# A hymba layer on one core: the job order of the attention projections, the queue of the backward scan's reloads, and the first two products

## The chip, the core and the metric

The kernel runs on one core of a Trainium2 chip. The metric is device microseconds (us) of one execution. Before the change three runs gave a median of 1325.76 us (1324.9 to 1326.83).

## What is computed

One encoder layer on 2048 tokens of width 1024, in float32. A single projection of the input feeds two mixers: neighbourhood attention with 8 heads on a grid of 32 rows and 64 columns, and a gated linear recurrence (HGRN2) with 4 heads that runs over the tokens in both directions. Both results are gated, put side by side, projected once more and added to the input, and a LayerNorm follows. Cut to that, the reference reads:

```python
h = jnp.einsum('btd,de->bte', x, w_in) + b_in
q_a, k_a, v_a, g_a, q_h, z_fwd, z_bwd, i_h, g_h = jnp.split(h, split_at, axis=-1)
o_a = neighbourhood_attention(heads_a(q_a), heads_a(k_a), heads_a(v_a), rpb)
o_a = o_a * jax.nn.silu(g_a)
logf_f, k_f = hgrn2_forget(heads_h(z_fwd), lb_fwd_logits, layer)
logf_b, k_b = hgrn2_forget(heads_h(z_bwd), lb_bwd_logits, layer)
o_fwd = hgrn2_chunk_scan(qh, k_f, ih, logf_f)
o_bwd = flip(hgrn2_chunk_scan(flip(qh), flip(k_b), flip(ih), flip(logf_b)))
o_h = rms_norm(o_fwd + o_bwd) * hg_norm_gain * jax.nn.silu(g_h)
y = jnp.einsum('bte,ed->btd', jnp.concatenate([o_a, o_h], axis=-1), w_out) + b_out
out = layer_norm(alpha * x + y)
```

## The kernel before

**Products.** Every float32 operand of a projection is split (`split`, L152) into a rounded high part, which ACT casts (L155), and a low part, which VectorE gets by a subtract (L156). A product is then three matmuls for each of 8 K-tiles: high by high, low by high, high by low. So a projection of one column chunk of 128 for one block of 512 tokens is 24 matmuls of 512 columns. The four value projections of a mixer go together in a wide job of 96 matmuls. All instructions of TensorE go through `mm` and `transpose` (L139, L142), which chain them in the order in which the code issues them.

**Units.** The tokens come in two halves of two blocks each (block 0 and 1, then 2 and 3). Each half has eight units: hg 0 to 3, one head of the recurrence each, then att 0 to 3, two heads of attention each. Numbered through they are n = 0 to 15; n = 8 to 11 are the hg units of the second half and n = 12 to 15 its attention units. An hg unit of the second half runs the forward scan, then the backward scan over all four blocks. For the blocks of the first half it reloads what it had stored in DRAM: `fetch` (L639 to L648) loads rQg, ub, op and rg, 256 KB each, for two blocks, by SP's queue. `hg_back` (L576) goes through a block in four steps: a matmul `pb` with the state `Sb`, and a step of `Sb` on VectorE (L586).

**Fillers.** The projections are not done in phases of their own. `projections` (L319) is a generator that yields after each matmul, and `advance` (L951) draws from it between the steps of the units, so that TensorE has work while other engines prepare the next step. Such a matmul is called a filler here; each half has 1728 of them, and 144 more come from the output projection (`out_first`, L914). The order of the fillers is that of the jobs (`half_jobs`, L282). How they spread is set by the table `marks` (L890): its entries say at which filler a unit starts, and within a unit the fillers are spread evenly over its steps (an attention unit of the second half has 45, three for each iteration). Weights are loaded by SP's queue and split when a job begins or the one ahead of it does (`prepare`, L323); at the start of the last job the first w_out tiles and features for the output product are loaded (`out_loads`, L910).

**An attention unit** has 12 items (`main`, L809). Each iteration does three things with fillers between them: the scores of an item (`scores`, L741: matmuls `S` of the split queries in `km` and `qm` and the split keys in `ST`, then the softmax on VectorE and ACT), the transposes `ptr` of the item two before (`turn`, L770), and on every second iteration the product with the values, `pov` (`weigh`, L784). Ahead of its first scores stand the splits of the queries and keys of its first group: `prep_q` (L698 to L709, casts on ACT, subtracts at L707 and L708 on VectorE) and `prep_k` (L716 to L723). For block 1 they read the reloads rq, r0k and r1k (L683 to L690, SP's queue). A unit checks whether it may start the splits of the next one (`ahead`, called at L821 from iteration 11 on, and at the end of hg units): that is when all q and k projections of the next unit have been issued.

**The start.** `first_loads` (L179) loads the weights of the chunks 16 (q) and 20 (zf) of the first hg unit and block 0 of the transposed input in halves of 256 columns; the first two products then run in two rounds of 256 columns, 96 matmuls in all (L341 to L352): all K-tiles of q, then all of zf, then both for the other half of the columns.

Of the kernel before, what the change touches and what calls it, by code (L numbers as in the profile page):

```python
# [11 lines left out]
F32 = mybir.dt.float32  # L12
F32R = mybir.dt.float32r
# [5 lines left out]
P = 128  # L19
# [3 lines left out]
TB = 512  # L23
NTB = T // TB
KT = D // P
ATT_HEADS, DH = 8, 64
HG_HEADS = 4
NCHUNK = 36
# [47 lines left out]
def _build():  # L76
    nc = _bacc.Bacc("TRN2", target_bir_lowering=False, num_devices=1, dynamic_dma_scratch_size=4096)

    def din(name, shape):
        return nc.dram_tensor("in_%s_dram" % name, shape, F32, kind="ExternalInput").ap()  # L80

    x_in = din("x", (T, D))
    xT_in = din("xT", (KT, P, T))
    w_in = din("w_in", (NCHUNK, P, KT, P))
    b_in = din("b_in", (P, NCHUNK))
    wv_in = din("w_v", (2, KT, P, 4 * P))
# [6 lines left out]
    out = nc.dram_tensor("out_0_dram", (T, D), F32, kind="ExternalOutput").ap()  # L93

    with tile.TileContext(nc) as tc, ExitStack() as top:
# [17 lines left out]
        def h_tile(name):  # L113
            return hp.tile([P, TB], F32, tag="h", name=name)
# [24 lines left out]
        def mm(out, lhsT, rhs, start, stop, **kw):  # L139
            in_order(nc.tensor.matmul(out, lhsT=lhsT, rhs=rhs, start=start, stop=stop, **kw))  # L140
# [10 lines left out]
        def split(dst, raw, scale=None):  # L151

            hi, lo = dst[:, 0], dst[:, 1]
            if scale is None:
                nc.scalar.copy(out=hi, in_=raw)  # L155
                last_split[0] = nc.vector.tensor_tensor(out=lo, in0=raw, in1=hi.bitcast(F32), op=ALU.subtract)  # L156
            else:
                nc.scalar.activation(hi, raw, AF.Copy, scale=scale)
                nc.vector.scalar_tensor_tensor(out=lo, in0=raw, scalar=scale, in1=hi.bitcast(F32), op0=ALU.mult, op1=ALU.subtract)
# [18 lines left out]

        def first_loads():  # L179


            wa = wp.tile([P, 2, KT, P], F32R, tag="w", name="wt")
            wraw = [rawp.tile([P, KT // 2, P], F32, tag="raw", name="wraw") for _ in range(2)]
            tiles = [xwp.tile([P, 2, TB], F32R, tag="xw", name="xt") for _ in range(KT)]

            def half(o, kt, n):
                cs = slice(o * 256, o * 256 + 256)
                raw = h_tile("xraw").rearrange("p (k t) -> p k t", k=2)
                nc.sync.dma_start(out=raw[:, 0:n], in_=xT_in[kt:kt + n, :, cs].rearrange("k p t -> p k t"))
                for k in range(n):  # L190
                    split(tiles[kt + k][:, :, cs], raw[:, k])

            for kt in range(0, KT, 2):
                part = wraw[kt // 4][:, kt % 4:kt % 4 + 2]
                nc.sync.dma_start(out=part, in_=w_in[16, :, kt:kt + 2])
                split(wa[:, :, kt:kt + 2], part)
                if kt == 0:
                    half(0, 0, 1)
                    half(0, 1, 1)
                else:  # L200
                    half(0, kt, 2)
            wb = load_w(20)
            for kt in range(0, KT, 2):
                half(1, kt, 2)
            return wa, wb, tiles

        def load_w(c):
            w = wp.tile([P, 2, KT, P], F32R, tag="w", name="wt")
            for i in range(2):
                raw = rawp.tile([P, KT // 2, P], F32, tag="raw", name="wraw")  # L210
                nc.sync.dma_start(out=raw, in_=w_in[c, :, i * 4:i * 4 + 4])
                split(w[:, :, i * 4:i * 4 + 4], raw, 0.125 if c < 4 else None)
            return w
# [66 lines left out]
        xts = {}  # L280

        def half_jobs(half):  # L282

            tbs = (0, 1) if half == 0 else (2, 3)
            first = 8 * half

            def both(u, *whats):
                hg = {"q": 16, "zf": 20, "zb": 24, "g": 32}
                att = {"q": 0, "k": 4, "g": 12}
                return [(first + u, what, (hg[what] + u) if u < 4 else (att[what] + u - 4), tb, (first + u, what))  # L290
                        for what in whats for tb in tbs]

            def wide(what, tb):
                return [(first, what, WIDE.index(what), tb, (what, tb))]

            jobs = both(0, "q", "zf", "zb")
            jobs[1], jobs[2] = jobs[2], jobs[1]
            jobs += wide("v4", tbs[0]) + wide("v4", tbs[1]) + both(0, "g")
            for u in (1, 2, 3):
                jobs += both(u, "q", "zf", "zb", "g")  # L300
            jobs += wide("a4", tbs[0]) + both(4, "q", "k") + wide("a4", tbs[1]) + both(4, "g")
            jobs += both(5, "q", "k", "g") + both(6, "q", "k", "g")
            end = both(7, "q", "k", "g")
            if half == 0:
                end[3], end[4] = end[4], end[3]
                return jobs + end
            end = [end[i] for i in (0, 2, 1, 3, 4, 5)]
            return jobs + [(n, what, c, tb, (n, what, tb)) for n, what, c, tb, _ in end]
# [10 lines left out]
        def projections():  # L319
# [18 lines left out]
            first_consts()  # L338
            prepare(jobs[2])
            banks = [ps_tile("pj", "pj"), ps_tile("pj", "pj")]  # L340
            for o in range(2):  # L341
                cs = slice(o * 256, o * 256 + 256)
                for ps, what in zip(banks, ("q", "zf")):
                    w = ws[0, what]
                    for kt in range(KT):
                        for i, (a, b) in enumerate(((0, 0), (1, 0), (0, 1))):
                            mm(ps[:, cs], w[:, a, kt], xts[0][kt][:, b, cs], kt == 0 and i == 0, kt == KT - 1 and i == 2)
                            if (kt * 3 + i) % 2 and not (o == 1 and kt == KT - 1 and i == 2):
                                yield 1
                    if o == 1:  # L350
                        gots[0][what, 0] = evac_plain(ps, 16) if what == "q" else evac_tanh(ps, 20)
                        yield 1  # L352
            for m, job in enumerate(jobs):
# [259 lines left out]
        def hg_unit(half, u, h, ahead):  # L613
# [25 lines left out]
            def fetch(tb):  # L639
                s = hg_saved[u, tb]  # L640
                Qg = h_tile("rQg")
                nc.sync.dma_start(out=Qg, in_=s["Qg"])
                ub = wk("ub", [P, 4, P], F32)
                nc.sync.dma_start(out=ub.rearrange("p a b -> p (a b)"), in_=s["ub"])
                op = wk("op", [P, 4, P], F32)
                nc.sync.dma_start(out=op.rearrange("p a b -> p (a b)"), in_=s["op"])
                g = h_tile("rg")
                nc.sync.dma_start(out=g, in_=gots[u]["g", tb])  # L648
                h["g", tb] = g
                rs[tb] = dict(Qg=Qg, ub=ub, op=op, dec=s["dec"])  # L650

# [236 lines left out]
        total = sum(job_size(job) for half in range(2) for job in half_jobs(half))  # L888
        half = total // 2
        marks = [240, 540, 772, 1004, 1240, 1425, 1610, 1795]  # L890
        marks += [half + 250, half + 540, half + 770, half + 1000, half + 1232, half + 1396, half + 1555, half + 1714, total + 144]

        def all_fillers():
            yield from projections()
# [240 lines left out]
```

## Time and profile before

| | us |
|---|---|
| median of 3 runs | 1325.76 |
| the profiled execution | 1326.96 |
| its span | 1325.2 |
| TensorE (PE) busy | 1300.8 |
| VectorE (DVE) busy | 877.9 |
| ScalarE (ACT) busy | 669.6 |
| GpSimd (POOL) busy | 92.0 |

What lies between the span and the execution's time is 1.8 us. Times are counted from the span's start. In the timeline a row is the start, the length, the engine, the line, the operation with its tiles and shapes, a count, and in brackets the idle time ahead of it with what ended it; SPq is SP's DMA queue. The end of a matmul is modelled, so a price is read from one start to the next. In the windows each engine has its busy time and instruction count, and behind them stand the granted TensorE clock (1.00 is full), the share of time that the DMA engines were busy, and GB/s. Groups give busy time and mean ns of one instruction, then the idle time ahead of them. DMA rows give the count, the size, and the median us from issue to landing.

TensorE is the busiest engine from the start to the end. From 1174 us on only the output product and the LayerNorm are left.

### The profile page before, as it was taken

The numbers are of one execution on the slowest core, as the hardware profiler recorded it, in microseconds if no ns is written. First come the engines' busy times: TensorE is split into PE (matmuls) and PEld (weight loads), VectorE is DVE, ScalarE is ACT, GpSimd is POOL, SyncE is SP. The second block draws the span as 40 slices with busy tenths as digits, with TensorE's granted clock in tenths as the row PEclk, the third lists the DMA queues.
The fourth block names the chain that finished last, engine by engine and source line by source line (L and its number), as shares of the span: only waits on it lengthen the run. The fifth ranks groups of instructions, "written<-read, shape, count | busy, mean of one in ns | idle before, by whom it ended". The sixth has DMA issues, their size and how long they took to land. (4 is left out here: it accounts for less than half of the span.)

```text
span 1325.2 us, 23230 instructions
## 1 busy us (share of the span) xinstructions
PE 1300.8 (98%) x8774; PEld 1088.3 (82%) x8774; DVE 877.9 (66%) x2078; ACT 669.6 (51%) x1426; POOL 92.0 (7%) x172
## 2 busy tenths in 40 slices
PE   9999999999999999999999999999999999999997
PEld 8888888888888888888888888878778787888886
DVE  4763656665544364764778868587484869789855
ACT  5443545545454464533646556467575879631000
POOL 0010000003120000010000002012000000000000
PEclk9999999999999999999999999999989999999999
DMA  7242222134353265242223233357435458466311
GB/s 223 91 149 72 90 73 82 57 114 141 112 156 103 88 188 168 81 151 73 74 72 98 72 104 124 107 180 228 143 116 158 133 191 266 141 228 216 143 40 64
DMA packets 101184, 169.33 MB, mean 128 GB/s; under 512 B 11408, under 2 KB 45456, under 8 KB 101072
## 3 DMA queue, kind: packets, MB, share of 16 engines
q1 hardware_dynamic: 91200, 138.61, 32.2%
q0 software_dynamic: 9728, 29.11, 6.5%
q8 instruction: 69, 1.13, 0.4%
q14 instruction: 43, 0.35, 0.1%
q10 hardware_dynamic: 144, 0.13, 0.0%
HBM read 130.31 MB, written 37.49 MB: 127 GB/s over the span
## 5 line engine op out<-in xcount | busy, mean ns | idle before, releaser
L140 PE MATMUL pj<-xt,wt 128*128 128x512 f32 (+1 forms) x2736 | 682.4, 397 | 1.0 <-ACT xt L155 0.4
L140 PEld LDWEIGHTS pj<-xt,wt 128*128 128x128 f32 x2736 | 495.0, 190 | 96.6 <-issue 3.8
L140 PE MATMUL pv<-wv,xt 128*128 128x512 f32 x768 | 191.7, 398 | 0.0
L140 PE MATMUL yp<-wo,chi 128*128 128x512 f32 (+1 forms) x528 | 162.3, 386 | 0.0
L140 PEld LDWEIGHTS pv<-wv,xt 128*128 128x128 f32 x768 | 139.9, 188 | 26.6 <-issue 0.3
L764 ACT ACTIVATE ub<-ub,nm 128x384 f32<-128x384 f32 (+2 forms) x128 | 78.7, 616 | 86.5 <-DVE nm L763 86.2
L513 ACT COPY km<-ST 128x512 f32<-128x512 f32 x96 | 64.3, 670 | 103.1 <-PE plev L140 45.7
L140 PEld LDWEIGHTS yp<-wo,chi 128*128 128x128 f32 x528 | 98.0, 189 | 19.4
L156 DVE TENSOR_TENSOR wt<-wraw,wt 128x512 fp32r<-128x512 f32 (+1 forms) x102 | 66.3, 677 | 44.1 <-ACT wt L155 42.4
L248 ACT ACTIVATE ht<-pj,bs_sb 128x512 f32<-128x512 f32 x64 | 43.9, 686 | 79.9 <-PE pj L140 79.5
L156 DVE TENSOR_TENSOR wv<-vraw,wv 128x512 fp32r<-128x512 f32 x64 | 41.7, 686 | 55.8 <-ACT wv L155 55.8
L524 DVE TENSOR_TENSOR ST<-ST,PX 128x512 f32<-128x512 f32 x96 | 66.0, 688 | 11.7 <-ACT qm L515 11.4
L780 ACT COPY op<-ptr 96x384 f32<-96x384 f32 (+3 forms) x128 | 60.7, 523 | 12.2 <-PE ptr L143 12.2
L525 DVE TENSOR_TENSOR ST<-ST,PX 128x512 f32<-128x512 f32 x96 | 65.7, 684 | 0.0
L155 ACT CAST wt<-wraw 128x512 fp32r<-128x512 f32 (+1 forms) x102 | 58.4, 612 | 13.1 <-issue 5.6
L515 ACT COPY qm<-ST 128x512 f32<-128x512 f32 x96 | 64.1, 668 | 0.0
L143 PE MATMUL ptr<-ident,ub 128*128 128x128 f32 (+1 forms) x448 | 59.8, 273 | 1.9 <-DVE rs L765 1.9
L143 PEld LDWEIGHTS ptr<-ident,ub 128*128 128x128 f32 (+1 forms) x448 | 51.6, 133 | 12.0 <-issue 2.1
L155 ACT CAST wv<-vraw 128x512 fp32r<-128x512 f32 x64 | 36.6, 617 | 39.5 <-PE pv L140 32.3
L766 DVE TENSOR_SCALAR ub<-ub,rs 128x384 f32<-128x384 f32 (+2 forms) x128 | 52.0, 421 | 2.9
L494 DVE COPY_PREDICATED AH<-masks,plev 128x256 f32<-128x256 uint8 x96 | 42.8, 446 | 15.1 <-PE plev L140 13.0
L140 PEld LDWEIGHTS plev<-qm,km 128*64 128x64 f32 x1536 | 47.5, 138 | 5.6 <-issue 4.9
(207 smaller groups left out, 1784.9 us busy)
## 6 DMA issues: line engine op xcount, KB each, us to landing
wraw<-in_w_in_dram SPq DMA_DIRECT2D x116, 256.0 KB, 3.1
vraw<-in_w_v_dram SPq DMA_DIRECT2D x64, 256.0 KB, 2.8
craw<-cat SPq DMA_DIRECT2D x32, 256.0 KB, 4.0
xraw<-in_xT_dram SPq DMA_DIRECT2D x31, 256.0 KB, 4.1
PP<-in_rpb_dram SPq DMA_DIRECT2D x16, 384.0 KB, 3.7
PX<-in_rpb_dram SPq DMA_DIRECT2D x16, 384.0 KB, 3.5
cat<-hu POOLq DMA_DIRECT2D x20, 256.0 KB, 2.9
vh<-hv POOLq DMA_DIRECT2D x16, 256.0 KB, 3.2
```

What stands on the lines that cost most here:

```text
L140: in_order(nc.tensor.matmul(out, lhsT=lhsT, rhs=rhs, start=start, stop=stop, **kw))
L143: in_order(nc.tensor.transpose(out=out, in_=in_, identity=ident))
L155: nc.scalar.copy(out=hi, in_=raw)
L156: last_split[0] = nc.vector.tensor_tensor(out=lo, in0=raw, in1=hi.bitcast(F32), op=ALU.subtract)
L248: nc.scalar.activation(t, ps, AF.Tanh, bias=bs_sb[:, c:c + 1], scale=0.5)
L513: nc.scalar.copy(out=km.rearrange("p (n h b) -> p n h b", h=2, b=B), in_=mix(ST, 0, 3, B, 0, TB))
L515: nc.scalar.copy(out=qm.rearrange("p (n h b) -> p n h b", h=2, b=B), in_=mix(ST, 1, 2, B, 0, TB))
L524: nc.vector.tensor_tensor(out=S1, in0=S1, in1=pr[:, :, :, 0].unsqueeze(3).to_broadcast([P, 2, m, B]), op=ALU.mult)
L525: nc.vector.tensor_tensor(out=S2, in0=S2, in1=pr[:, :, :, 1].unsqueeze(3).to_broadcast([P, 2, m, B]), op=ALU.mult)
L764: nc.scalar.activation(sb[:, 0:nk], sb[:, 0:nk], AF.Exp, bias=nm, scale=-1.0, accum_out=sums[:, hd:hd + 1])
L766: nc.vector.tensor_scalar(out=sb[:, 0:nk], in0=sb[:, 0:nk], scalar1=rs[:, hd:hd + 1], scalar2=None, op0=ALU.mult)
L780: nc.scalar.copy(out=PT[0:n, 0:nch].rearrange("p a b -> p (a b)"), in_=pt[0:n, 0:nch * P])
```

## The change

There are four edits.

1. **The start.** A new input `w0` holds the chunks 16 and 20 beside each other for each pair of K-tiles. `first_loads` now loads, for each pair, 256 KB of `w0` and two K-tiles of 512 columns of x, 256 KB each. The two products run side by side, K-tile by K-tile, with 48 matmuls of 512 columns.
2. **Jobs.** In both halves the gate job of unit att 0 for the second block moves behind the q jobs of att 1, so the order is now: gate of the first block, q of att 1 (both blocks), gate of the second block, k of att 1. For that the two gate jobs have keys of their own, and their weights are loaded and split twice.
3. **Reloads.** The four kinds of reload in `fetch` go by GpSimd's queue.
4. **Starts.** In the second half the units 11 to 15 start at the fillers 990, 1215, 1436, 1588 and 1731 (counted from the half's first) instead of 1000, 1232, 1396, 1555 and 1714.

```diff
@@ inputs
+    w0_in = din("w0", (KT // 2, P, 2, 2, P))
@@ first_loads
-            wa = wp.tile([P, 2, KT, P], F32R, tag="w", name="wt")
-            wraw = [rawp.tile([P, KT // 2, P], F32, tag="raw", name="wraw") for _ in range(2)]
-            tiles = [xwp.tile([P, 2, TB], F32R, tag="xw", name="xt") for _ in range(KT)]
-
-            def half(o, kt, n):
-                cs = slice(o * 256, o * 256 + 256)
-                raw = h_tile("xraw").rearrange("p (k t) -> p k t", k=2)
-                nc.sync.dma_start(out=raw[:, 0:n], in_=xT_in[kt:kt + n, :, cs].rearrange("k p t -> p k t"))
-                for k in range(n):
-                    split(tiles[kt + k][:, :, cs], raw[:, k])
-
+            ws = [wp.tile([P, 2, KT, P], F32R, tag="w", name="wt") for _ in range(2)]
+            tiles = []
             for kt in range(0, KT, 2):
-                part = wraw[kt // 4][:, kt % 4:kt % 4 + 2]
-                nc.sync.dma_start(out=part, in_=w_in[16, :, kt:kt + 2])
-                split(wa[:, :, kt:kt + 2], part)
-                if kt == 0:
-                    half(0, 0, 1)
-                    half(0, 1, 1)
-                else:
-                    half(0, kt, 2)
-            wb = load_w(20)
-            for kt in range(0, KT, 2):
-                half(1, kt, 2)
-            return wa, wb, tiles
+                raw = h_tile("wraw").rearrange("p (c k f) -> p c k f", c=2, k=2)
+                nc.sync.dma_start(out=raw, in_=w0_in[kt // 2])
+                for c, w in enumerate(ws):
+                    split(w[:, :, kt:kt + 2], raw[:, c])
+                for k in range(2):
+                    raw = h_tile("xraw")
+                    nc.sync.dma_start(out=raw, in_=xT_in[kt + k, :, 0:TB])
+                    t = xwp.tile([P, 2, TB], F32R, tag="xw", name="xt")
+                    split(t, raw)
+                    tiles.append(t)
+            return ws[0], ws[1], tiles
@@ half_jobs
-            jobs += wide("a4", tbs[0]) + both(4, "q", "k") + wide("a4", tbs[1]) + both(4, "g")
-            jobs += both(5, "q", "k", "g") + both(6, "q", "k", "g")
+            jobs += wide("a4", tbs[0]) + both(4, "q", "k") + wide("a4", tbs[1])
+            gates = [job[:4] + ((job[0], "g", job[3]),) for job in both(4, "g")]
+            jobs += gates[:1] + both(5, "q") + gates[1:] + both(5, "k")
+            jobs += both(5, "g") + both(6, "q", "k", "g")
@@ projections
-            for o in range(2):
-                cs = slice(o * 256, o * 256 + 256)
+            for kt in range(KT):
                 for ps, what in zip(banks, ("q", "zf")):
                     w = ws[0, what]
-                    for kt in range(KT):
-                        for i, (a, b) in enumerate(((0, 0), (1, 0), (0, 1))):
-                            mm(ps[:, cs], w[:, a, kt], xts[0][kt][:, b, cs], kt == 0 and i == 0, kt == KT - 1 and i == 2)
-                            if (kt * 3 + i) % 2 and not (o == 1 and kt == KT - 1 and i == 2):
-                                yield 1
-                    if o == 1:
+                    for i, (a, b) in enumerate(((0, 0), (1, 0), (0, 1))):
+                        mm(ps, w[:, a, kt], xts[0][kt][:, b], kt == 0 and i == 0, kt == KT - 1 and i == 2)
+                        if not (kt == KT - 1 and i == 2):
+                            yield 1
+                    if kt == KT - 1:
@@ hg_unit, fetch: each of the four reloads
-                nc.sync.dma_start(out=Qg, in_=s["Qg"])
+                nc.gpsimd.dma_start(out=Qg, in_=s["Qg"])
...
@@ marks
-        marks += [half + 250, half + 540, half + 770, half + 1000, half + 1232, half + 1396, half + 1555, half + 1714, total + 144]
+        marks += [half + 250, half + 540, half + 770, half + 990, half + 1215, half + 1436, half + 1588, half + 1731, total + 144]
```

Line numbers of the changed kernel are about 10 lower. The first place that the prediction speaks of is VectorE between units 12 and 13. The rows begin with the last reloaded keys of unit 13's first group (`ST<-r1k`); `hp` are projections as ACT evacuated them, `km` and `qm` the split queries, here those of its second group, and the instruction that reads `S` is the reduction of the first scores. Before:

```order
L723 TENSOR_TENSOR ST<-r1k,ST 64x256 x4
L723 TENSOR_TENSOR ST<-hp,ST 64x256
L707 TENSOR_TENSOR km<-hp,km 64x512
L763 ISA ub,nm<-S,PX 128x384
L763 ISA nm 128x1
L708 TENSOR_TENSOR km<-hp,km 64x512
L763 ISA ub,nm<-S,PX 128x384
L763 ISA nm 128x1
L765 RECIPROCAL rs<-sums 128x1
L707 TENSOR_TENSOR qm<-hp,qm 64x512
```

After:

```order
L713 TENSOR_TENSOR ST<-r1k,ST 64x256 x4
L713 TENSOR_TENSOR ST<-hp,ST 64x256
L697 TENSOR_TENSOR km<-hp,km 64x512
L698 TENSOR_TENSOR km<-hp,km 64x512
L245 SCALAR_TENSOR_TENSOR hu<-ht,hu 128x512
L697 TENSOR_TENSOR qm<-hp,qm 64x512
L698 TENSOR_TENSOR qm<-hp,qm 64x512
L713 TENSOR_TENSOR ST<-hp,ST 64x256 x4
L784 SCALAR_TENSOR_TENSOR hu<-pov,b_sb,hu 128x8x32
L753 ISA ub,nm<-S,PX 128x384
L753 ISA nm 128x1
```

The second group's splits, some of which stood behind the first two reductions, now all stand ahead of the first one, with two steps of the gates between them.

The second place is the reloads of hg unit 3 in the second half (n = 11), before on SP's queue:

```order
L644 DMA ub<-sub_1_3623 128x512
L644 DMA ub<-sub_0_3299 128x512
L642 DMA rQg<-sQg_1_3621 128x512
L648 DMA rg<-sg_1_2806 128x512
L642 DMA rQg<-sQg_0_3297 128x512
L648 DMA rg<-sg_0_2738 128x512
L646 DMA op<-sop_1_3625 128x512
L646 DMA op<-sop_0_3301 128x512
L220 DMA vraw<-in_w_v_dram 128x512
L683 DMA rq<-sq_3629 128x512
L688 DMA r0k<-sk_3633 128x256
```

After, on GpSimd's queue, behind the last stores of the values (`vt`) ahead of them:

```order
L407 DMA vt_5_124<-hv 64x256 x2
L407 DMA vt_5_132<-hv 64x256 x2
L632 DMA rQg<-sQg_1_3557 128x512
L638 DMA rg<-sg_1_2742 128x512
L632 DMA rQg<-sQg_0_3233 128x512
L638 DMA rg<-sg_0_2674 128x512
L634 DMA ub<-sub_1_3559 128x512
L634 DMA ub<-sub_0_3235 128x512
L636 DMA op<-sop_1_3561 128x512
L636 DMA op<-sop_0_3237 128x512
```

The eight reloads have left SP's queue, where they stood between loads of values (`vt`) and the next weights, rq and r0k, and follow the stores of the fifth value tile on GpSimd's.

The third place is TensorE between units 14 and 15, from the last fillers ahead of unit 15's first scores on; `yp` is the output product. Before:

```order
L140 MATMUL pov<-op,A 64x128 x4
L140 MATMUL pov<-op,ks 64x128 x2
L140 MATMUL pj<-xt,wt 128x512 x4
L140 MATMUL S<-ST,km 128x384 x2
L140 MATMUL S<-ST,qm 128x384 x2
L140 MATMUL pj<-xt,wt 128x512 x10
L140 MATMUL S<-ST,km 128x512 x2
L140 MATMUL S<-ST,qm 128x512 x2
L140 MATMUL pj<-xt,wt 128x512 x4
L140 MATMUL yp_11707<-wo,chi 128x512 x2
L140 MATMUL yp_11707<-wo,clo 128x512
```

After:

```order
L141 MATMUL pov<-op,ks 64x128 x2
L141 MATMUL pov<-op,A 64x128 x4
L141 MATMUL pov<-op,ks 64x128 x2
L141 MATMUL pj<-xt,wt 128x512
L141 MATMUL yp_11615<-wo,chi 128x512 x2
L141 MATMUL yp_11615<-wo,clo 128x512
L141 MATMUL S<-ST,km 128x384 x2
L141 MATMUL S<-ST,qm 128x384 x2
L141 MATMUL yp_11615<-wo,chi 128x512 x2
L141 MATMUL yp_11615<-wo,clo 128x512
L141 MATMUL yp_11615<-wo,chi 128x512 x2
```

Unit 15's first scores stood ahead of the first `yp`, with 14 projection matmuls between; now three `yp` matmuls stand ahead of them.

More of the change, by code (lines that the diff above doesn't have):

```diff
@@ L641, in fetch @@
                 Qg = h_tile("rQg")
-                nc.sync.dma_start(out=Qg, in_=s["Qg"])
+                nc.gpsimd.dma_start(out=Qg, in_=s["Qg"])
                 ub = wk("ub", [P, 4, P], F32)
-                nc.sync.dma_start(out=ub.rearrange("p a b -> p (a b)"), in_=s["ub"])
+                nc.gpsimd.dma_start(out=ub.rearrange("p a b -> p (a b)"), in_=s["ub"])
                 op = wk("op", [P, 4, P], F32)
-                nc.sync.dma_start(out=op.rearrange("p a b -> p (a b)"), in_=s["op"])
+                nc.gpsimd.dma_start(out=op.rearrange("p a b -> p (a b)"), in_=s["op"])
                 g = h_tile("rg")
-                nc.sync.dma_start(out=g, in_=gots[u]["g", tb])
+                nc.gpsimd.dma_start(out=g, in_=gots[u]["g", tb])
                 h["g", tb] = g
@@ L1121 @@
         "xT": np.ascontiguousarray(x2.T).reshape(KT, P, T),
+        "w0": np.ascontiguousarray(
+            w_in[0].reshape(KT // 2, 2, P, NCHUNK, P)[:, :, :, [16, 20]].transpose(0, 2, 3, 1, 4)),
         "w_in": np.ascontiguousarray(w_in[0].reshape(KT, P, NCHUNK, P).transpose(2, 1, 0, 3)),
```

## The prediction

> **What bounds the kernel now.** I read the page first: the busy shares, then the waits of TensorE, then its timeline and the windows around each wait.
>
> ```profile
> PE 1300.8 (98%) x8774; PEld 1088.3 (82%) x8774; DVE 877.9 (66%) x2078; ACT 669.6 (51%) x1426; POOL 92.0 (7%) x172
> ...
> PE S L140 <- DVE ST L723: 8.5, 4, 5.9
> PE pb L140 <- DVE Sb L586: 2.8, 4, 1.9
> PE ptr L143 <- DVE rs L765: 1.9, 1, 1.9
> ...
> PE pk L143 <- DVE ST L525: 0.7, 2, 0.4
> ```
>
> TensorE is busy for 98% of the span, so an edit can gain only where TensorE waits or runs at a lower clock. The waits (total, times, longest) name three places: the scores `S` wait for the keys' split `ST`, the backward scan's `pb` waits for its state `Sb`, and once the transposes `ptr` wait for the softmax. A busy TensorE still hides a start that is fed too slowly and stretches at half clock; the windows show both (length, then busy time of PE, PEld, DVE, ACT, POOL, then the granted clock, the DMA share and GB/s).
>
> ```profile
> 0.00:6.30 6.30, 5.11 (x13) 4.14 (x14) 1.90 (x6) 2.84 (x5) 0.91 (x8) 1.00 0.54 175
> 6.30:12.10 5.80, 4.76 (x28) 3.55 (x26) 3.74 (x10) 4.09 (x10) 0.00 (x0) 1.00 0.96 303
> 9.10:12.50 3.40, 2.36 (x14) 1.59 (x13) 2.34 (x5) 2.33 (x7) 0.00 (x0) 1.00 1.02 359
> 12.50:15.90 3.40, 3.40 (x18) 3.40 (x17) 3.36 (x11) 2.55 (x9) 0.00 (x0) 0.50 1.05 338
> ```
>
> From 6.3 to 12.1 us DMA is at its limit (0.96 to 1.02 of its time) and TensorE gets 28 matmuls done; then a window of 3.4 us follows at half clock.
>
> **A. The start.** The rows are TensorE's first products, the evacuation of the second one, and a later stretch in which nothing holds 512-column matmuls up.
>
> ```profile
> 6.34 3.13 PE L140 MATMUL pj<-xt,wt 128*128 128x256 f32 x18
> 9.89 1.20 PE L140 MATMUL pj<-xt,wt 128*128 128x256 f32 x6 [0.42 <-ACT xt L155]
> ...
> 22.39 0.69 ACT L248 ACTIVATE ht<-pj,bs_sb 128x512 f32<-128x512 f32 x1
> ...
> 875.22 11.38 PE L140 MATMUL pv<-wv,xt 128*128 128x512 f32 x49
> 886.44 0.52 PE L140 MATMUL S<-ST,km 128*128 128x384 f32 x2
> ```
>
> Before, 96 matmuls of 256 columns take from 6.34 to 22.39, 16.05 us. After, there are 48 of 512 columns; the undisturbed price is (886.44 - 875.22) / 49 = 0.229 us, so 11.0 us if the data is there: at most 5.05 us gained. Is it there? The new order needs twelve loads of 256 KB, 3.15 MB. By 6.3 us 175 GB/s have brought 1.10 MB, enough for the first weights and two K-tiles of x; the other 2.04 MB take 5.7 to 6.7 us at the 359 to 303 GB/s of the rows, so the last lands at 12 to 13 us and, with a cast and a subtract (0.62 and 0.69 us, rows below), is ready by 14.3. Its six matmuls are due at 6.34 + 42 x 0.229 = 16.0. So the end isn't bound by data; the first K-tiles are, since each now brings twice the bytes of its columns. I leave 0.65 us for two such waits (a first one was 0.42). The half-clock window should go, as TensorE is fed between 9 and 12.5 us. **A = -4.4, between -3.5 and -5.05.**
>
> **B. The reloads by GpSimd's queue.** Thirty-two loads of 256 KB leave SP's queue. The rows are the last hg unit's: its first rQg reload, the attention unit's rq behind all eight, and what follows.
>
> ```profile
> 859.93 0.43 SPq L642 DMA_DIRECT2D rQg<-sQg  x1
> ...
> 863.55 0.38 SPq L683 DMA_DIRECT2D rq<-sq  x1
> ...
> 867.59 0.38 PE L140 MATMUL pb<-Sb,rQg 128*128 128x128 f32 x2
> ...
> 869.30 0.62 ACT L705 CAST km<-rq 64x512 fp32r<-64x512 f32 x1 [1.88 <-DMA rq<-sq]
> ...
> 870.96 0.49 PE L140 MATMUL pb<-Sb,rQg 128*128 128x128 f32 x2 [0.24 <-DVE Sb L586]
> ...
> 873.86 0.49 PE L140 MATMUL pb<-Sb,rQg 128*128 128x128 f32 x2 [1.95 <-DVE Sb L586]
> ...
> 874.98 0.49 PE L140 MATMUL pb<-Sb,rQg 128*128 128x128 f32 x2 [0.40 <-DVE Sb L586]
> ...
> 860.00:870.00 10.00, 10.00 (x65) 8.91 (x64) 6.23 (x16) 5.06 (x16) 0.00 (x0) 1.00 0.96 334
> ```
>
> rq is issued at 863.55 and used at 869.30, in a window with DMA at 0.96; VectorE's `km<-rq` waits for it with the rest of the `Sb` chain behind, and TensorE loses 0.24 + 1.95 + 0.40 = 2.6 us. With the eight reloads off SP, rq can go out up to 3.6 us earlier (863.55 - 859.93). The bytes are the same, and the new order still puts `km<-rq` between the `Sb` steps, so part may stay: **B = -1.8, between 0 and -2.6.** The price on GpSimd is bounded by rows of that queue.
>
> ```profile
> 892.86 6.51 POOL L417 DMA_DIRECT2D vt<-hv  x12 [3.69 <-ACT hv L413]
> ...
> 890.00:900.00 10.00, 9.98 (x56) 7.79 (x55) 9.64 (x28) 5.93 (x14) 6.56 (x13) 1.00 0.73 228
> ...
> cat<-hu POOLq DMA_DIRECT2D x20, 256.0 KB, 2.9
> ...
> rQg<-sQg SPq DMA_DIRECT2D x8, 256.0 KB, 4.9
> ```
>
> Twelve issues took 6.51 us, 0.54 each, with VectorE busy for 9.64 of 10 us; eight reloads are then 4.3 us of a queue that is busy for 7% of the span. GpSimd's 256 KB stores land in 2.9 us, SP's reloads in 4.9. The first `pb` that reads rQg comes 7.7 us after the issue (867.59 - 859.93): 0.54 + 4.9 fits, so I add nothing for this. The Trainium skill ("SBUF — State Buffer", the box on the "DVE blocks DMA" trap in "SBUF: two separate sides") says that a DMA issued by GpSimd has its descriptors written by that engine's cores, which VectorE in a two-port mode locks out, and advises SP or ACT. That speaks against this edit; the row of 0.54 us an issue under a full VectorE shows no such lock here.
>
> **C. Into attention unit 13.** The rows are the first scores of units 13 and 14, with the windows of the clock.
>
> ```profile
> 963.72 1.01 PE L140 MATMUL S<-ST,km 128*128 128x384 f32 x2 [5.93 <-DVE ST L723]
> ...
> 958.00:961.40 3.40, 0.00 (x0) 0.00 (x0) 3.31 (x6) 3.23 (x8) 0.40 (x1) 1.00 0.91 288
> 961.40:964.80 3.40, 1.08 (x3) 0.80 (x4) 3.18 (x9) 3.28 (x8) 0.00 (x0) 0.50 0.32 102
> 964.80:968.20 3.40, 3.40 (x9) 2.82 (x9) 3.27 (x10) 3.14 (x8) 0.00 (x0) 0.50 0.10 18
> ...
> 1035.29 0.62 PE L140 MATMUL S<-ST,km 128*128 128x384 f32 x2 [2.11 <-DVE ST L723]
> ...
> 1033.10:1036.50 3.40, 1.12 (x5) 0.72 (x5) 3.22 (x8) 3.29 (x7) 0.00 (x0) 1.00 0.63 180
> 1036.50:1039.90 3.40, 3.40 (x10) 2.72 (x9) 3.16 (x11) 3.31 (x9) 0.54 (x1) 0.50 0.45 136
> ...
> L723 DVE TENSOR_TENSOR ST<-hp,ST 64x256 fp32r<-64x256 f32 x56 | 23.2, 419 | 16.3 <-ACT ST L722 15.1
> L707 DVE TENSOR_TENSOR km<-hp,km 64x512 fp32r<-64x512 f32 x12 | 8.2, 680 | 1.9 <-ACT km L705 1.9
> L156 DVE TENSOR_TENSOR wt<-wraw,wt 128x512 fp32r<-128x512 f32 x98 | 64.6, 687 | 41.1 <-ACT wt L155 39.5 <-PE pov L140 1.2
> ...
> L155 ACT CAST wt<-wraw 128x512 fp32r<-128x512 f32 x98 | 56.8, 621 | 11.3 <-issue 5.6 <-PE pv L140 4.3 <-ACT qm L515 0.6
> ...
> L764 ACT ACTIVATE ub<-ub,nm 128x384 f32<-128x384 f32 (+2 forms) x128 | 78.7, 616 | 86.5 <-DVE nm L763 86.2
> ```
>
> TensorE waits 5.93 us for the split; afterwards 1.08 + 3.40 us of work run at half clock, of which half, 2.24, is lost: 8.2 us. The split can't start before unit 13's last k product, filler 1392 of the second half in both programs (g, q, g, k are as many fillers as g, g, q, k). What changes is unit 13's start, 1396 before and 1436 now. Unit 12's iterations check for the split at fillers 1215 + 221 x 36/45 = 1391.8 (a hair too early) and, three 45ths later, 1406, so it starts with 30 fillers ahead of the first `S`: 30 x 0.229 = 6.9 us, and some 2 us of transposes and `pov`. The split up to the keys is 4 x 0.68 + 7 x 0.42 = 5.7 us of VectorE, with a cast of 0.62 ahead and one gate step beside it: about 7. It fits. **C = -8.2, and -4.5 if casts of other tiles push the split back by half its cover.**
>
> **D. Into unit 14.** Start 1555 becomes 1588. The wait of 2.11 and half of 3.40 us at half clock go, 3.8 us, as 41 fillers (9.4 us) now lie between the check at 1436 + 152 x 33/45 = 1547 and the scores, against 11 before (1396 + 159 x 42/45 = 1544, the first check behind the last k product at 1536). **D = -3.8, between -2 and -3.8.** The Trainium skill ("TensorE: Matmul & The Clock Gate", "Why this matters for your kernels") asks for no idle gaps over about 3 us, and by that the wait of 2.11 would cost no clock and D would be -2.1, the sum 1.7 us smaller. The rows differ: a window with 1.12 us of work in 3.40 was followed by half clock.
>
> **E. Into unit 15.** Start 1714 becomes 1731, behind filler 1728, so the output product's first matmuls `yp` stand ahead of unit 15's first scores instead of behind. The rows: where TensorE waited in that unit, and the load there.
>
> ```profile
> 1115.00 0.61 PE L143 MATMUL ptr<-ident,ub 128*96 128x128 f32 x4 [1.88 <-DVE rs L765]
> ...
> 1100.00:1110.00 10.00, 10.00 (x63) 8.13 (x63) 9.56 (x19) 9.71 (x20) 0.00 (x0) 1.00 0.83 255
> ```
>
> VectorE and ACT are full for those 10 us with the splits of w_out, of the concatenated features and of unit 15's keys. The 1.88 may go, as these come earlier against the scores. But the first `yp` need w_out and the features, loaded from filler 1704 on, and what lies between loses unit 15's first two scores (eight matmuls, some 2 us by the row of 886.44); units 13 and 14 also have 7 and 16 fillers fewer to cover the same vector work. I take 0: **E between -1.9 and +3.**
>
> **F. Small costs.** The gates' weights of unit 4 are now loaded and split twice a half: two casts and two subtracts, 2.6 us a half beside TensorE's work, which hides them. Units 10 and 11 give 220 and 225 fillers instead of 230 and 232, so scan waits like the 0.7 us on `pk` can double. **F = +0.8, between 0 and +1.5.**
>
> **The sum.** -4.4 - 1.8 - 8.2 - 3.8 + 0 + 0.8 = -17.4. The profiled execution took 1326.96 us: 1309.6. It lies 1.2 over the median of the runs (1325.76), so on their level 1308.4. With all terms at their best -21.4, 1304.4; at their worst -5.5, 1320.3.
>
> **The rivals.**
> 1. *The stalls move* (0.17). Behind the first `km<-rq` VectorE's new order holds 8 steps of 0.68, 11 of 0.42 and three gate steps before the reduction of unit 13's first scores, 10.1 us and with the gate steps (0.5 to 0.7 each) about 12; the softmax after it, with an exponential of 0.62 a head between two steps of VectorE, is some 2.5. From the check at 1406 to the first `ptr` (7 of 45 steps into unit 13's 152 fillers, 1459) TensorE has 53 fillers (12.1 us) and the first scores and transposes, about 16 in all, before it needs that. The margin is under 2 us with ACT as full as in C's windows. If half of C's wait returns at the `ptr` (+3), B gives nothing (+1.8) and E costs 3 and a half-clock window (+4.7): 1308.4 + 9.5 = 1317.9. For it speaks the load of 0.95 in both engines; against it that the same vector work then has more TensorE work beside it.
> 2. *Slower: the reloads come late* (0.04). GpSimd's queue goes in order; unit 11's reloads stand behind the `vt` stores, which wait for ACT's copies, and buffers that free late block it. Each of four units would hold its `pb` chain. To undo 17.4 us and add 2.7, each must lose 5 us: the first rQg would land 7.7 + 5 = 12.7 us after 859.93, instead of some 5. If it were 14, the time is 1308.4 + 4 x 6.3 - 1.8 of B = about 1332. Against it: 0.54 an issue and 2.9 to 4.9 to landing.
> 3. *It doesn't do what it says* (0.03). The split may still wait past filler 1436, for a k product that ACT evacuates late or for rq, while E costs 3 and the start stays bound by DMA: then A -1.5, C and D together -2, E +3, F +0.8: +0.3, within 0.2% of before, 1326.
> 4. *More goes* (0.04). E gains its 1.9 and softmax waits inside the longer unit 12 vanish: 1304 or less.
>
> **How the numbers follow.** The forecast has 0.72, at 1308.4. What a measurement can tell from no change is about 0.2%, 2.65 us. The range reaches up to rival 1 and down past the best sum, 1303.5 to 1318. Faster by over 0.2%: 0.72 + 0.17 + 0.04 = 0.93; same 0.03; slower 0.04.
>
> **What would show it.** A: the second product's evacuation near 18.0, no half clock before 16 us. B: SP's rq ahead of 861, no wait for `Sb` over 1 us. C and D: no wait of `S` for `ST` and full clock into units 13 and 14. E: at most 2 us of wait at the first `yp`. It is wrong if `pb` waits for a DMA (rival 2), if `ptr` waits for `rs` at the start of unit 13 by over 2 us (rival 1), or if `S` still waits for `ST` (rival 3).

## The result and the profile after

The changed kernel takes 1313.13 us (median of 4 runs, 1312.59 to 1314.86) against 1325.49 (4 runs, 1324.9 to 1326.83): a ratio of 0.9908, with an interval of 0.989 to 0.9925. That is 12.4 us less; the forecast was 17.4 less. The profiled execution has a span of 1310.8 us, 14.4 less than that of before.

First the page's busy row and TensorE's waits after the change (total, times, longest).

```profile
PE 1295.1 (99%) x8726; PEld 1081.1 (82%) x8726; DVE 879.4 (67%) x2076; ACT 671.4 (51%) x1424; POOL 109.9 (8%) x204
...
PE S L141 <- DVE ST L713: 1.2, 2, 0.9
PE warm L141 <- DVE eps L1016: 1.2, 1, 1.2
PE S L141 <- DVE hu L597: 1.2, 1, 1.2
PE pk L144 <- DVE ST L515: 1.1, 3, 0.5
PE ptr L144 <- DVE rg L784: 0.8, 1, 0.8
PE pb L141 <- DVE Sb L576: 0.6, 2, 0.4
PE yp L141 <- ACT chi L927: 0.4, 1, 0.4
```

The scores' waits for `ST` fell from 8.5 to 1.2 us, those of `pb` from 2.8 to 0.6, and the wait of `ptr` for the softmax (`rs`) is gone. In their place stand several waits of about 1 us: the scores wait once for `hu`, 1.2 us, in unit 12, and what is left of their waits for `ST` lies inside unit 15. The windows of the start and of the 20 us around unit 15's start have the columns explained above.

```profile
6.30:12.10 5.80, 5.80 (x27) 4.80 (x26) 5.21 (x11) 5.28 (x12) 0.00 (x0) 1.00 1.04 381
9.10:12.50 3.40, 3.40 (x17) 2.82 (x16) 3.40 (x8) 3.19 (x8) 0.00 (x0) 1.00 1.07 378
12.50:15.90 3.40, 3.40 (x17) 2.82 (x16) 2.70 (x7) 2.28 (x5) 0.00 (x0) 1.00 1.04 381
1090.00:1100.00 10.00, 9.57 (x52) 7.26 (x49) 8.81 (x21) 9.66 (x20) 0.54 (x1) 1.00 0.87 275
1100.00:1110.00 10.00, 8.48 (x45) 6.61 (x44) 8.08 (x25) 8.33 (x19) 0.00 (x0) 1.00 0.71 234
```

At the start TensorE is busy throughout, and DMA brings 378 to 381 GB/s where it brought 303 to 359. In unit 15 TensorE does wait: it is busy for 9.57 and 8.48 of 10 us. The timeline shows the start and the split ahead of unit 13.

```profile
6.24 18.00 PE L141 MATMUL pj<-xt,wt 128*128 128x512 f32 x76
...
18.48 0.69 ACT L238 ACTIVATE ht<-pj,bs_sb 128x512 f32<-128x512 f32 x1
...
950.72 0.63 ACT L695 CAST km<-rq 64x512 fp32r<-64x512 f32 x1
...
957.30 0.42 DVE L713 TENSOR_TENSOR ST<-hp,ST 64x256 fp32r<-64x256 f32 x1
...
962.57 0.51 PE L141 MATMUL S<-ST,km 128*128 128x384 f32 x2
...
940.00:970.00 30.00, 30.00 (x201) 24.84 (x201) 21.67 (x54) 21.72 (x50) 1.09 (x2) 1.00 0.49 155
1020.00:1040.00 20.00, 20.00 (x119) 16.70 (x118) 16.52 (x45) 14.57 (x34) 0.54 (x1) 1.00 0.44 141
```

The second product's evacuation starts at 18.48 instead of 22.39, behind that of the first product, which now ends together with it; TensorE's next filler starts at 17.6 instead of 22.2. The split into unit 13 runs from 950.72 to 957.72, 7.0 us, and the scores come 4.9 us after it without a wait. The two windows around the starts of units 13 and 14 show TensorE busy all the time at full clock.

**Where the time went.** A filler is a matmul that can be found in both traces, so I read off when each unit's first filler starts, and compare the stretches between. Where a table moved a unit's start, the fillers that a stretch has more or fewer are taken out at 0.2285 us each. The columns are what each stretch lost (+) or gained (-) against the profiled execution of before, in us. Each row is one execution. "Start" is the time up to the filler behind the first two products (48 slots of 512 columns); units 0 to 9 are one column and hold the fillers ahead of unit 0 too. A unit's first scores stand ahead of its first filler, so the wait into unit 13 counts in the column of unit 12.

| kernel | start | 0-9 | 10 | 11 | 12 | 13 | 14 | 15 | sum |
|---|---|---|---|---|---|---|---|---|---|
| the change | -4.59 | +0.08 | +0.53 | -1.01 | -6.17 | -4.25 | -1.04 | +2.16 | -14.30 |
| e1, start alone | -4.85 | +0.02 | 0.00 | -0.25 | -0.07 | +0.29 | -0.01 | +0.28 | -4.57 |
| e2, table alone | -2.19 | +0.02 | +0.54 | -1.03 | -6.22 | -4.25 | -1.08 | +2.01 | -12.20 |
| e3, jobs alone | -0.34 | +0.63 | -0.01 | +1.03 | -0.06 | +0.48 | +0.01 | -0.71 | +1.01 |
| e4, reloads alone | -2.04 | +0.23 | -0.01 | -0.07 | -0.08 | -0.04 | -0.07 | -0.01 | -2.10 |
| before, once more | -2.10 | +0.06 | 0.00 | +0.75 | -1.19 | -0.29 | -0.48 | -0.29 | -3.55 |
| e11, unit 13 at 1416 | -3.90 | +0.04 | +0.53 | -1.00 | -2.26 | -4.10 | -0.57 | +1.96 | -9.32 |
| e12, units 11, 12 old | -3.72 | +0.02 | +0.01 | -0.03 | -7.72 | -4.25 | -0.80 | +3.02 | -13.48 |
| e7, unit 15 at 1714 | -4.30 | +0.12 | +0.53 | -1.04 | -6.22 | -4.25 | -0.02 | +4.50 | -10.68 |
| e8, early gate | -4.96 | +0.10 | +0.53 | -1.00 | -6.21 | -4.25 | +0.64 | -1.26 | -16.41 |
| e9, and early w_out | -4.21 | +0.05 | +0.53 | -0.98 | -6.21 | -4.25 | -0.45 | +1.32 | -14.20 |
| e10, three edits | -4.43 | +0.05 | +0.52 | -1.03 | -6.21 | -4.25 | +0.87 | -0.95 | -15.41 |
| e13, gate and old 11, 12 | -4.32 | +0.46 | +0.01 | -0.08 | -8.14 | -4.25 | +2.55 | -1.43 | -15.20 |

### The profile page after: what moved, and what is told of

Same layout as the page of the kernel before. It is cut to its first block, busy times and chain, and to the rows that moved or that the text cites. A ratio compares the mean times of both kernels' runs of the same rounds, so it can differ in the third digit from the quotient of the medians.

```text
span 1310.8 us, 23152 instructions
## 1 busy us (share of the span) xinstructions
PE 1295.1 (99%) x8726; PEld 1081.1 (82%) x8726; DVE 879.4 (67%) x2076; ACT 671.4 (51%) x1424; POOL 109.9 (8%) x204
## 4 chain that ended last, share of the span: by engine, by line
PE 91%; DVE 4%; ACT 3%; DMA 2%; issue 1%; DVEq 0%; ACTq 0%
PE pj L141 46%; PE yp L141 13%; PE pv L141 11%; PE plev L141 4%; PE pov L141 4%; PE ptr L144 3%; PE S L141 3%; PE po L141 2%; PE pk L144 1%; PE pub L141 1%; PE pu L141 1%; PE pb L141 1%; ACT ST L712 0%; DVE ub L753 0%; DMA ST<-in_vecs_dram 0%
## 5 line engine op out<-in xcount | busy, mean ns | idle before, releaser
L141 PE MATMUL pj<-xt,wt 128*128 128x512 f32 x2688 | 677.0, 398 | 0.1
L141 PEld LDWEIGHTS pj<-xt,wt 128*128 128x128 f32 x2688 | 488.0, 188 | 95.1 <-issue 3.9
L245 DVE SCALAR_TENSOR_TENSOR hu<-ht,hu 128x512 f32<-128x512 f32 x32 | 22.1, 691 | 46.1 <-ACT hu L244 46.0
```

## The experiments

**Each edit alone.** My theory after the result: the start gives its 4.6, the table all that units 12 to 15 show, the job order and the reloads next to nothing. The rivals: the job order carries unit 13, and the reloads carry unit 11.

*e1, the start alone:* `w0`, `first_loads` and the two products as in the change, all else as before.

> The kernel before with the new start alone (w0, 512-column products side by side). Theory, from the two traces: the first two products end 4.6 us earlier and everything behind them is only shifted, so the time falls by 4.6 (4 to 5), to about 1320.9. Rival (the gain at the start is given back, because a shifted phase of loads or of the clock's windows costs it later): under 2 us.

1323.61 us against 1325.33, ratio 0.9987 (0.9978 to 0.9996): 1.7 us, 0.5 to 2.9. That is less than the theory's, and the rival's number is met, but its reason isn't seen in the trace: behind the start the stretches of its trace add up to +0.3. The size came from elsewhere, as the traces of e2 and e4 and a second profile of before show below.

*e2, the table alone:*

```diff
-half + 1000, half + 1232, half + 1396, half + 1555, half + 1714
+half + 990, half + 1215, half + 1436, half + 1588, half + 1731
```

> The kernel before with the new table of unit starts alone; old job order, reloads on SP, old start. Theory: both job orders finish the last k product of unit 13 at filler 1392, so the table alone removes the waits into units 13 and 14 and pays at unit 15: -7.6 - 3.8 + 2.2, about -9, so about 1316.5. Rival (the job order carries it): with the old order the split into unit 13 is still late, the wait of S for ST there stays over 3 us, and the gain is under 5.

1314.76 us, ratio 0.9915 (0.9901 to 0.9928): 10.6 us, 1.6 more than the theory's. Its stretches from unit 10 on are those of the whole change to within 0.15 us each, without the new jobs and with the reloads on SP. TensorE's waits in it:

```profile
PE S L140 <- DVE ST L723: 1.2, 2, 0.9
PE warm L140 <- DVE eps L1026: 1.2, 1, 1.2
PE S L140 <- DVE hu L607: 1.1, 1, 1.1
PE pk L143 <- DVE ST L525: 1.0, 3, 0.4
PE ptr L143 <- DVE rg L794: 0.8, 1, 0.8
PE pb L140 <- DVE Sb L586: 0.7, 3, 0.4
```

The same rows as after the change, almost to the number. The rival falls: the table does it.

*e3, the jobs alone:*

```diff
-jobs += wide("a4", tbs[0]) + both(4, "q", "k") + wide("a4", tbs[1]) + both(4, "g")
-jobs += both(5, "q", "k", "g") + both(6, "q", "k", "g")
+jobs += wide("a4", tbs[0]) + both(4, "q", "k") + wide("a4", tbs[1])
+gates = [job[:4] + ((job[0], "g", job[3]),) for job in both(4, "g")]
+jobs += gates[:1] + both(5, "q") + gates[1:] + both(5, "k")
+jobs += both(5, "g") + both(6, "q", "k", "g")
```

> The kernel before with the new job order alone (the gate of unit att 0 split into two jobs with two loads of its weights); old starts. Theory: the order alone changes nothing at filler 1392, within 1 us of before, with the wait of 5.9 us into unit 13 still there. Rival (the job order carries it): the wait into unit 13 falls by over 3 us and the time with it. A cost of the doubled weights would show as +1 or more.

1326.84 us, ratio 1.0008 (0.9999 to 1.0017). The rival falls: the waits of S for ST are still 8.2 us in all, 5.9 the longest. The median is 1.5 us over before and the ratio's interval, -0.1 to +2.3 us, just includes no difference, so a cost of the doubled weights isn't excluded by the time. The trace shows none where the weights are loaded: the first of the two loads falls into units 0 to 9, whose +0.63 lies ahead of unit 0, and the second into unit 12 (-0.06). Units 11 and 13 lost 1.5 with the same waits as before; in unit 11 half clock followed its wait (shown at the end), which it didn't in before.

*e4, the reloads alone:*

```diff
-nc.sync.dma_start(out=Qg, in_=s["Qg"])
+nc.gpsimd.dma_start(out=Qg, in_=s["Qg"])
...
```

> The kernel before with the four kinds of reload on GpSimd's queue alone. The forecast on record: -1.8, by the 2.6 us of waits of pb for Sb in the last scan. Theory after seeing the trace of the change, where units 10 and 11 together gave 0.4 us: waits of pb for Sb fall from 2.8 to about 1 and something of the same size takes their place, so -0.5 (0 to -1.5). Rival (reloads on GpSimd come late): slower by over 1, with waits of pb for a DMA.

1324.74 us, ratio 0.9995 (0.9987 to 1.0004), and no stretch from unit 10 on moved by more than 0.08 us. The rows of the last scan, and the reloads' landing:

```profile
860.48 0.38 SPq L683 DMA_DIRECT2D rq<-sq  x1
...
863.46 0.62 ACT L705 CAST km<-rq 64x512 fp32r<-64x512 f32 x1 [1.99 <-DMA rq<-sq]
...
869.38 0.46 PE L140 MATMUL pb<-Sb,rQg 128*128 128x128 f32 x2 [0.43 <-ACT pb L594]
...
871.40 0.49 PE L140 MATMUL pb<-Sb,rQg 128*128 128x128 f32 x2 [1.10 <-DVE Sb L586]
...
rQg<-sQg POOLq DMA_DIRECT2D x8, 256.0 KB, 6.3
```

On the span's clock rq is issued 3.1 us earlier and cast 5.8 us earlier; 1.8 of each is this execution's shorter start, so the queue is worth 1.3 and 4.0. It bought nothing: VectorE now takes more of unit 12's splits between the `Sb` steps, and from one start to the next TensorE's gaps there still add up to 3.0 us (3.2 in before), in five pieces instead of three. The reloads land in 6.3 us instead of 4.9, still in time: on GpSimd's queue unit 11's first `rQg` goes out at 829.7 us, 36 us ahead of the first `pb` that reads it.

**Was it cover?** Theory: the wait into unit 13 is the split's chain less the work between the first possible check and the scores.

*e11, unit 13 in between:* `half + 1436` becomes `half + 1416` in the changed kernel.

> The changed kernel with unit 13's start at 1416, between the 1396 of before and its own 1436. Theory (the wait into unit 13 is the split's chain less the work that stands between the first check behind filler 1392 and the scores): the check falls at 1403, so 13 fillers and the last pov, about 4.5 us, cover a split of 6.3 and the evacuation ahead of it; a wait of S for ST of about 2 to 2.5 us returns, and with it up to 2 us of half clock: 1315 to 1317.5. Rival (the wait went for another reason, the reloads' queue or the job order): no wait over 0.5 us there and the changed kernel's time, 1313.

1316.6 us, ratio 0.9931 (0.9917 to 0.9945), 3.5 over the change, within what was expected. The wait is back, but smaller than I worked out. The split's first cast and the first scores in e11:

```profile
955.94 0.63 ACT L695 CAST km<-rq 64x512 fp32r<-64x512 f32 x1
...
962.03 0.62 PE L141 MATMUL S<-ST,km 128*128 128x384 f32 x2 [0.98 <-DVE ST L713]
...
962.82 0.62 PE L141 MATMUL S<-ST,qm 128*128 128x384 f32 x2 [0.17 <-DVE ST L713]
```

The cast in before, whose scores start at 963.72 behind 5.93 us of waiting:

```profile
957.47 0.62 ACT L705 CAST km<-rq 64x512 fp32r<-64x512 f32 x1
```

In before TensorE runs out of work at 957.79, 0.3 us after the split's first cast; in e11 at 961.05, 5.1 us after it (the fillers behind the check at 1403 and the last `pov`). So 4.8 us more of work stand beside the split, and the wait is 4.8 us shorter: in sum 1.15 us at 1416 and none at 1436, against 5.93 at 1396. Cover is what counts. The rest of the 3.5 us isn't this wait. The profiled execution, the slowest of the five at 1318.38 us, has a stretch at half clock from 890.9 to 894.4 us, behind a wait of 1.15 us for `hu`, which cost about 1.8 us; the change has the same wait (1.16) without half clock.

*e12, units 11 and 12 as before:* `half + 990, half + 1215` become `half + 1000, half + 1232` in the changed kernel.

> The changed kernel with the starts of units 11 and 12 back at 1000 and 1232 and the others as changed. In the trace of the change unit 10 lost 0.5 and unit 11 gained 1.0 us against before, and in the kernel with the table alone too. Theory: the earlier starts carry these, so unit 11 loses its 1.0 again and unit 10 its 0.5 gain, and unit 12 has 17 fillers fewer beside the same work: within 1.5 us of 1313. Rival (the earlier start of unit 12 is what gives the room ahead of unit 13): over 2 us slower, with a wait of S for ST into unit 13.

1312.44 us, ratio 0.9905 (0.989 to 0.9919). Unit 11's gain of 1.0 and unit 10's loss go, and `pb` waits 1.5 us as in e4. So unit 11's gain in the change came with the earlier starts of units 11 and 12 (both were moved, so which of them isn't shown), not from the queue. Unit 12 gains 1.5 more instead: the wait of its scores for `hu`, 1.2 us in the change, isn't there. No wait returns ahead of unit 13, so the rival falls.

**Unit 15.** Theory: unit 15 lost 2.2 us because the first `yp` stand ahead of its scores. Rivals: it is when the splits of w_out fall, or how much vector work of all kinds falls there.

*e7, unit 15 back:* `half + 1731` becomes `half + 1714` in the changed kernel.

> The changed kernel with unit 15's start back at filler 1714. Theory: unit 15 lost 2.2 us against before because the output product's first matmuls came ahead of its scores while VectorE and ACT were full; with 1714 these matmuls stand behind the scores again and unit 15 gets 158 fillers, so 1 to 2 us come back: about 1311.5. Rival (unit 14, left with 126 fillers, or the old wait of ptr takes it back): no faster, 1313 to 1315.

1315.74 us, ratio 0.9923 (0.9911 to 0.9935), 2.6 over the change. My theory falls: with `yp` behind the scores unit 15 loses 4.5 us, not 2.2, and unit 14 no longer gains its 1.0.

```profile
PE ptr L144 <- ACT op L770: 3.0, 3, 1.4
PE yp L141 <- ACT chi L927: 2.1, 2, 1.2
```

*e8, an early gate,* and *e9, with the first half of w_out a job earlier as well:*

```diff
-            end = [end[i] for i in (0, 2, 1, 3, 4, 5)]
+            end = [end[i] for i in (0, 2, 4, 1, 3, 5)]
...
+                if m == len(jobs) - 2:
+                    load_wo(0)
                 if m == len(jobs) - 1:
-                    out_loads()
+                    first_half.append(load_cat(0))
```

> The changed kernel with the gate of unit 15's first block as third instead of fifth of the last six jobs. It is the control for the next one: TensorE's work is the same, so within 1 us of the changed kernel by both theories, about 1313.

> As the one with the early gate, and the first half of w_out is loaded and split one job (24 fillers) earlier, before the features are. Theory (unit 15 loses its 2 us to sixteen splits that all fall into the 20 us around its start): with eight of them 5.5 us earlier the waits there fall and 1 to 2 us are gained, about 1311.5. Rival (it is the order of yp before the scores, whatever the load): the waits stay and the time too, about 1313.

e8 takes 1311.39 us, ratio 0.9889 (0.9875 to 0.9903), where I had expected no difference; e9 takes 1312.7, ratio 0.99 (0.9884 to 0.9916), where I had expected a gain. The waits of e9 and of e8:

```profile
PE ptr L144 <- ACT op L772: 2.1, 1, 2.1
```

```profile
PE ptr L144 <- ACT op L770: 1.2, 1, 1.2
PE pov L141 <- ACT op L770: 1.2, 2, 0.6
```

With the gate two jobs earlier unit 15 gains 1.3 us on before instead of losing 2.2, and unit 14 loses 0.6 instead of gaining 1.0: 1.7 us better than the change in sum. With half of w_out earlier as well, unit 15 is 2.6 worse than in e8 and unit 14 1.1 better. The two other kernels with the early gate (e10 and e13, below) show the same exchange: unit 15 gains 1.0 and 1.4, unit 14 loses 0.9 and 2.6. What TensorE waits for in each is ACT's copy of the transposed weights (`op`) or a split, that is, its turn on an engine that is busy for 9.66 and 8.33 of 10 us in the windows of the change. The order in which that work comes seems to decide; which single step does isn't settled.

*Before, profiled once more.*

> The kernel before once more, for its profile alone. The profile of before showed half clock from 12.5 to 15.9 us and its 48 slots of the first two products ended at 22.2; two kernels with the same start ended them at 20.0 and 20.2 without half clock. Theory (the half clock there comes and goes from one execution to the next): either 22.2 with half clock or 20.0 without, and nothing between.

1323.4 us, and the second product's evacuation starts at 20.29. Its start, in windows:

```profile
6.30:12.10 5.80, 5.11 (x31) 3.97 (x30) 4.23 (x11) 4.55 (x12) 0.00 (x0) 1.00 0.99 325
9.10:12.50 3.40, 3.04 (x19) 2.47 (x20) 3.04 (x8) 2.88 (x8) 0.00 (x0) 1.00 1.08 372
12.50:15.90 3.40, 3.40 (x31) 3.40 (x30) 2.76 (x9) 2.50 (x7) 0.00 (x0) 1.00 1.05 362
```

The same program had 2.36 us of work in the second window of the first profile and half clock in the third; here it has 3.04 and full clock. The old start was profiled five times: half clock in two (before, e3), full in three (e2, e4, this one), and these three end it 1.7 to 2.2 us earlier. In e2 and e4 TensorE has 2.85 and 2.92 us of work in the second window; in e3 half clock begins at 11.3 us, behind 3.4 us with 2.26 of work.

**Together.** *e10: the start, the table and the early gate,* without the new jobs and with the reloads on SP; *e13: the change with the early gate and units 11 and 12 as before.*

> The kernel before with the new start, the new table of unit starts and the early gate of unit 15's first block; the old job order around att 1 and the reloads on SP's queue. Theory (the split gate jobs and GpSimd's reloads are worth nothing, and the rest adds up): the time of the changed kernel with the early gate, 1311.4, within 1 us. Rival (they are worth something once the table is there): slower than that by over 1.5.

> The changed kernel with the early gate of unit 15's first block and the starts of units 11 and 12 back at 1000 and 1232: the two edits that looked best, together. By the segments of their traces the gate gives 1.7 us in units 14 and 15, and the old starts 1.1 in units 10 to 12. Theory (the segments add): 1310.3, about 1 us under the kernel with the early gate alone (1311.4). Rival (unit 15's loss with the old starts, 3.0 instead of 2.2 us, comes from them and stays): 1311.4 or more.

e10 takes 1311.72 us, ratio 0.9898 (0.9884 to 0.9912), e8's time within 0.4: within what the runs can tell, two of the four edits can be left out. e13 takes 1310.4 us, ratio 0.9883 (0.9862 to 0.9905). That is the theory's number, but before took 1324.7 beside it: against that the gain is 14.3 us, and e8's against its own before (1325.66) is 14.3 too, so the runs don't show that the two add. By its trace they don't: units 10 to 12 gain 1.5 against e8, and unit 14 loses 1.9, where `pov` waits 2.0 us in sum (1.2 in e8) and half clock follows, which e8 doesn't have.

```profile
1093.00:1097.00 4.00, 4.00 (x13) 3.42 (x12) 3.49 (x6) 3.89 (x8) 0.00 (x0) 0.57 0.76 216
```

e13 and e8 beat before for certain; the 1.7 to 2.7 us by which they beat the change lie within overlapping intervals.

## Why the prediction was right, and where its sizes were off

The time fell inside the range, at 12.4 us less instead of 17.4, and the largest part, C and D, came by the mechanism forecast. B's mechanism failed, and A and E had the wrong size.

- **A (-4.4), the term that was mis-sized in the runs.** In the profiles it came out as predicted: the next filler starts 4.59 us earlier, and the second product's evacuation at 18.48 where "near 18.0" stood. What failed is the step "96 matmuls of 256 columns take from 6.34 to 22.39": that was one execution. In three of five the old start takes some 2 us less, at full clock. Against those the new start, in nine executions, gains 1.5 to 2.9, and alone it measured 1.7 (0.5 to 2.9). Taking the half clock as part of the old start's price cost the forecast about 2 to 2.7 us. Over all five old starts the new one gains 3.0 in the mean, just above that interval; how often the half clock comes in executions without a profile isn't known.
- **B (-1.8).** It is 0 (e4: unit 11 -0.07). The step "rq can go out up to 3.6 us earlier" held in its direction (1.3 us by the queue); that it shortens the `Sb` chain didn't. The bound at 0 was the right one, for the reason given with it: VectorE has the same steps to do between.
- **The price of GpSimd's queue.** 0.54 us an issue was taken and 0.55 came, and no `pb` waited for a DMA; rival 2 falls. The landing grew from 4.9 to 6.3 us in e4, to 6.6 in the change. It cost nothing because the reloads now go out much earlier: the last unit's first `rQg` at 828.4 us in the change, 32 us ahead of its first `pb`, where the forecast had set it against the 7.7 us of SP's queue. The Trainium skill ("SBUF — State Buffer", the box on the "DVE blocks DMA" trap) lets transfers from this queue wait while VectorE runs in a two-port mode. The longer landing agrees in sign; the runs don't show its cause.
- **C and D (-12.0 together).** Units 12 to 14 gained 11.5, and in e2 the same by the table alone. The chain of "about 7" was 7.0. The clock's part was right: no half clock is left there (1.00 in both windows above). The Trainium skill's rule that asks for no gaps over about 3 us ("TensorE: Matmul & The Clock Gate", "Why this matters for your kernels") doesn't agree with the runs: shorter gaps can cost clock too, and need not (below).
- **E (0, up to +3).** Unit 15 lost 2.2. The range held it, the value taken didn't: "the 1.88 may go" was right (it is gone), but waits on `yp`, `S` and `ptr` took its place, up to 0.9 us each and 3.0 in the unit's list against 2.2 in before. Read from one start to the next they cost more than the list says, by my reading about 4.7 us against 2.7. This is the other mis-sized term. The early gate takes unit 15's loss away (e8, e10, e13), in part at unit 14's expense; which wait makes it stays open.
- **F (+0.8).** Units 10 and 11 together gave -0.5. The denser scan wasn't the cost that I took it for; unit 11 even gained 1.0 by the table, where the listed waits of `pb` are 2.0 us shorter. In e2, with the reloads still on SP, the cast of `rq` no longer waits for its load either (1.88 us in before). Why the earlier starts do this isn't settled.
- Rival 1 happened in part (E), without B's and C's share of it: `ptr` doesn't wait at the start of unit 13. Rival 3 falls, as no wait of S for ST is left ahead of units 13 and 14, and rival 4 with E.
- Two sums of the forecast are off without moving it: the best terms as stated give -21.55 and not -21.4, and rival 2's 1332 takes B's 1.8 off a time that holds it already (1308.4 + 4 x 6.3 = 1333.6).

So of 5.0 us too much, A explains about 2 to 2.7, E 2.2, B 1.8 and C and D 0.5, and F, which was better by 1.3, takes some back: 5.2 to 5.9 in all.

## What to carry to other kernels

When one engine is busy for 98% of the span, look for the few places where it waits in front of a chain that could have begun earlier, and count the work between the moment at which the chain can begin and the one at which its result is needed: here a start 20 matmuls later put 4.8 us more of work beside the chain and took 4.8 us off the wait, and one line with five numbers gave 10.6 of the 12.4 us of a change of four edits. A transfer that lands earlier was worth nothing here, where the engine behind it had the same steps left. And a price read from one execution needs a second one wherever the clock changed in it.

## What the runs showed of the hardware

The same gap can cost clock in one execution and not in the next. In before, `pb` waits 1.95 us up to 873.86 and TensorE works for 0.74 us of three:

```profile
872.00:875.00 3.00, 0.74 (x4) 0.43 (x4) 2.89 (x7) 2.89 (x10) 0.00 (x0) 1.00 0.31 98
875.00:878.00 3.00, 3.00 (x14) 2.54 (x15) 2.85 (x6) 2.90 (x11) 0.00 (x0) 1.00 0.40 132
```

In e3, with the same wait (1.93) and 1.04 us of work, the three us behind it run at half clock:

```profile
872.00:875.00 3.00, 1.04 (x6) 0.73 (x6) 2.89 (x7) 2.89 (x11) 0.00 (x0) 0.99 0.42 124
875.00:878.00 3.00, 3.00 (x9) 2.40 (x8) 2.85 (x7) 2.90 (x12) 0.00 (x0) 0.50 0.33 106
```

The Trainium skill ("TensorE: Matmul & The Clock Gate", "What's actually happening") says that the clock's window of about 3.4 us runs freely; that fits a gap that counts or not by where it falls in the window, and it may be part of why runs of before lie between 1323 and 1330 us. The waits of 5.9 us into unit 13 came with half clock in all five executions of the old table that were profiled, and the waits of 2.1 us into unit 14 were followed by it in all five.
